# Storing raw z and its silu later, and passing q, k, v and 1/sum through DRAM in copies of 128 partitions

## The chip, the cores and the metric

The kernel runs on one core of a Trainium2 chip. The metric is the device time of one execution in microseconds (us). A core has a matrix engine (TensorE, PE in the profile, its weight loads PEld), a vector engine (VectorE, DVE), a scalar engine with lookup tables for functions such as exp and silu (ScalarE, ACT), a general engine (GpSimd, POOL) and SyncE (SP), which here only issues DMA copies. Sixteen DMA engines carry the copies between DRAM and the on-chip memory. Each engine follows its own list of instructions in order and waits for others by semaphores.

## The reference

One layer of a latent backbone, for 1,024 tokens (a grid of 16 rows by 64 columns), 256 context tokens, 1,024 features and 8 heads of 64, all in float32:

```python
h  = rmsnorm(x, norm_g) * (1 + scale) + shift          # scale, shift, gate from c and w_ada
hc = rmsnorm(ctx, norm_g) * (1 + scale_c) + shift_c
q, k, v, za, u, bg, cg, zc = jnp.split(h @ w_in, SPLIT_POINTS, axis=-1)     # 8 x 512 columns
kc, vc = jnp.split(hc @ w_in[:, D_ATTN:3 * D_ATTN], 2, axis=-1)
# q, k, kc: rmsnorm per head, q also rotated (axial rope) for the scores against k
# each query sees an 8 x 16 window of keys with a learned bias, and all 256 context keys
# without bias and with the unrotated q; one softmax over both
attn = neighbourhood_attention(q, k, v, kc, vc, rpb) * jax.nn.silu(za)
conv = bg * centred_short_conv(cg * u, conv_w, conv_b) * jax.nn.silu(zc)    # 3 taps
x_new = x + gate * (jnp.concatenate([attn, conv], axis=-1) @ w_out)
```

## The kernel before

Every product of matrices is done three times over (`mm3`): both operands are split into a high part and a rest, and high x high, high x rest and rest x high are added up. So q, k and v exist as two tensors each, index `l` (0 high, 1 rest). Work runs in four stages.

1. Modulation: `w_ada` is read, the gains and shifts are formed, x is normalised and turned so that features lie on partitions, and the products of the first group of the convolution are made.
2. Projection. The heads are handled in 4 pairs, 128 columns of q, k and v each. The loop `for n in range(NT + 3)` (L1170; NT = 32, a pair times a block of 128 tokens) issues one block's 24 matmuls into `pacc` and, behind it, the steps of the blocks before: normalisation, rotation, the transposes in `turn_qk` (L226) that put a pair's 2 x 64 head dimensions on the 128 partitions, and the stores. `turn_qk` stores q and k of two blocks at a time, `turn_kc` (L269) the context's keys and values. A store goes through `spill` into the list `stores`, which is emptied onto SP once a block. Each head has DRAM tensors of its own: `q_d[h]` holds q in both parts, rotated and plain, for 64 head dimensions, `k_d[h]` and `kc_d[h]` high part and rest of the keys, `v_d[h]` and `vc_d[h]` the values. So a pair's 128 partitions are stored by two copies of 64.
3. Attention. `quarter(n)` (L1066) runs for n = 0 to 35, four quarters a head and four more to finish. In one quarter, step by step, n's scores and context scores are made, n - 1's maxima are finished, n - 2's exponentials are taken, n - 3's products with v are summed. Scores have the keys on partitions; maxima over keys are found by transposes into `pmx`, `mx` before and `mg` after them. v has a column of ones behind its 64 (zeros in the rest), so that the same matmul gives the softmax's sums. `finish` (L1038) puts a half head's result into `o_d[p]` and its sums into `rs_d[p]`, by ScalarE's own queue.
   In between, TensorE does matmuls that attention doesn't need: the generator `fill` makes the z columns of the four head pairs (`attn_group`, L484), then three groups of the convolution (`conv_group`). `TICKS[n]` says how many portions go into quarter n; one portion is six matmuls of 512 columns into `pu`. Their weights come as `uraw` (two buffers, loaded a unit ahead by SP), are split on ScalarE (`uh`) and VectorE (`ul`). Work of theirs for ScalarE and VectorE is queued with `chore` and done at fixed places of a quarter by `do_acts` and `do_dves`.
   When a pair's last half is done, `gated(p)` (L1267) is made the current gating: a step in each quarter, run by `next(gating[0])`, inverts the sums by way of `ri_d[p]`, loads silu(z) (`zs`), the attention result (`tb`) and the inverse sums repeated over 64 partitions each (`rb`), multiplies, and stores `y_d[p]`. The last pair is gated in stage 4.
4. Output projection: `put_y` (L1334) loads the eight parts of y, `load_wo` the weights; 16 tiles of 24 matmuls into `pout`.

What a head loads for attention is asked for by `load_k`, `load_q` and `load_v` (from L944): the partitions 0 to 63 and 64 to 127 of `k_s` and of `kc_s` are both filled with the head's 64 rows, in which high part and rest of the keys lie side by side. `q_s` has the high part of q on partitions 0 to 63 and the rest on 64 to 127 (i below), and in its free dimension the rotated q ahead of the plain one (k below), so that one matmul multiplies a part of the keys with both parts of q:

```python
for i in range(2):
    rows = slice(64 * i, 64 * i + 64)
    for k in range(2):
        sp.dma_start(self.q[rows, k].bitcast(F32).rearrange("p (t c) -> p t c", c=256), q_d[h][i, :, :, k])
    sp.dma_start(self.kc[rows].bitcast(F32), kc_d[h])
```

So each tile of 128 partitions is filled by copies of 64. k and q have two sets of buffers, one for the even heads (`hcp`), one for the odd ones (`prp`). Head 0's k and q are loaded at the projection's blocks 26 and 27, each later head's during the head before: masks and q are asked for ahead of that head's quarter 1, k ahead of its quarter 2 (counted from 0), and v ahead of the own quarter 0.

In attention PE, ACT, DVE and POOL do their instructions in the order of the program (`strict`). The order on SP, and of all engines in the projection, is set by a scheduler that goes by a timing model of its own. All hardware copies of SP and ACT share eight semaphores.

Of the kernel before, what the change touches and what calls it, by code (L numbers as in the profile page):

```python
# [39 lines left out]
def body(tc, es, x, ctxt, w_ada, b_ada, w_in, q_g, k_g, rpbr, w_out, vecs, cst, out):  # L40
# [60 lines left out]
    zs_d = many("zs_d", NPAIR, [P, T])  # L101


    q_d = many("q_d", NH, [2, HD, 4, 2, 256])
    k_d = many("k_d", NH, [HD, 4, 2, 256])
    v_d = many("v_d", NH, [P, 4, 2, 2 * HD])
    kc_d = many("kc_d", NH, [HD, 2, L])
    vc_d = many("vc_d", NH, [P, 2, 2 * HD])
# [82 lines left out]

    def put_v(vs, i, ps):

        halves(vs[:, :, 0, i], vs[:, :, 1, i], ps.rearrange("p (s d) -> p s d", s=2))
# [31 lines left out]
    def turn_qk(pp, p, two, t0):  # L226
# [8 lines left out]
        def put():  # L235
# [4 lines left out]
            for s in range(2):  # L240
                h, rows = 2 * p + s, slice(64 * s, 64 * s + 64)
                for l in range(2):
                    spill(q_d[h][l, :, t0 // 2], qs[rows, l])
                spill(k_d[h][:, t0 // 2], ks[rows])
# [13 lines left out]
    def normed_ctx(pp, acc, scales):  # L258
        two = []
        vs = pp.tile([P, 2, 2, 2, HD], F32R, name="vs", tag="vs", bufs=4)  # L260
# [8 lines left out]
    def turn_kc(pp, p, two, vs):  # L269
# [4 lines left out]
        def put():  # L274
            ks = pp.tile([P, 2, 256], F32R, name="ks", tag="ks", bufs=2)
            halves(ks[:, 0], ks[:, 1], pB[:, :256])
            for s in range(2):
                h, rows = 2 * p + s, slice(64 * s, 64 * s + 64)
                spill(kc_d[h], ks[rows])
                spill(vc_d[h], vs[:, s].rearrange("p l i d -> p l (i d)"))  # L280
# [195 lines left out]

    def silus(z):
        out = []
        for half, ps in z:
            out.append(cvp.tile([P, 512], F32, name="zs", tag="ub", bufs=2))  # L480
            act.activation(out[half], ps, AF.Silu)
        return out

    def attn_group(f):  # L484

        z = []
        for got in unit(z_col(f)):
            if got:
                z.append(got)
            else:  # L490
                yield

        def on_act():
            for half, zs in enumerate(silus(z)):
                sp.dma_start(zs_d[f][:, half * 512:(half + 1) * 512], zs)
        chore(on_act)
# [8 lines left out]
    def load_sums(f, half, rb, queue):  # L505
        for i in range(2):
            queue.dma_start(rb[64 * i:64 * i + 64],
                            ri_d[f][i:i + 1, half * 512:(half + 1) * 512].broadcast_to([64, 512]))
# [426 lines left out]

    class head:
# [7 lines left out]
        def load_k(self):  # L944
            h = self.h
            self.k = self.place().tile([P, 4, 2, 256], F32R, name="k_s", tag="A")
            for i in range(2):
                sp.dma_start(self.k[64 * i:64 * i + 64].bitcast(F32), k_d[h])

        def load_q(self):  # L950
# [3 lines left out]
            for i in range(2):  # L954
                rows = slice(64 * i, 64 * i + 64)
                for k in range(2):
                    sp.dma_start(self.q[rows, k].bitcast(F32).rearrange("p (t c) -> p t c", c=256), q_d[h][i, :, :, k])
                sp.dma_start(self.kc[rows].bitcast(F32), kc_d[h])

        def load_v(self):  # L960
            h = self.h
            self.v = vts[h % 2]
            for l in range(2):
                for t in range(4):
                    sp.dma_start(self.v[:, l, 2 * t:2 * t + 2, 0:HD].bitcast(F32),
                                 v_d[h][:, t, l].rearrange("p (b d) -> p b d", d=HD))
                sp.dma_start(self.v[:, l, NB:, 0:HD].bitcast(F32), vc_d[h][:, l].rearrange("p (b d) -> p b d", d=HD))
# [98 lines left out]
    def quarter(n):  # L1066
# [17 lines left out]
        if gating and next(gating[0], "end"):  # L1084
            gating.clear()
# [5 lines left out]
        for i, hd_, j in now:  # L1091
            hd_.scores(j, sbank[:, i])
        if live(n):
# [11 lines left out]
        for _ in range(1):  # L1105
# [27 lines left out]
        for _ in range(ticks - 1):  # L1133
# [24 lines left out]
    sq = pp.tile([P, 4, HD + 1], F32, name="sq")  # L1158
    pool.memset(sq[:, :, HD:], EPS)
# [10 lines left out]
    for n in range(NT + 3):  # L1170
# [13 lines left out]
        if 9 <= n < 25 and n % 2:  # L1184
            next(tables)
        if n == NT - 6:
# [24 lines left out]
        if 0 < n <= NT:  # L1211
            scales[n - 1] = head_scale(pp, tiles[n - 1], 4)
            if n % 2:
                vs = pp.tile([P, 2, 2, 2, HD], F32R, name="vs", tag="vs", bufs=4)
# [228 lines left out]
```

## Time and profile before

| | before |
|---|---|
| median of 3 timed runs | 641.58 us (641.37 to 641.83) |
| profiled execution, whole | 643.59 us |
| its span, first to last instruction | 641.8 us |
| granted TensorE clock | 0.999 of full |
| TensorE busy | 629.1 us, 98% (weight loads 537.3 us, beside it) |
| VectorE busy | 432.3 us, 67% |
| ScalarE busy | 322.5 us, 50% |
| GpSimd busy | 131.5 us, 20% |
| SP's queue (q1) | 112,348 packets, 113.23 MB, 61.4% of 16 DMA engines |
| ScalarE's queue (q10) | 6,208 packets, 11.05 MB, 5.5% |
| DRAM read, written | 88.01 MB, 38.53 MB |

The profile is of one execution. Busy is time in which an engine carried out an instruction. An instruction made in a helper has the helper's line (L55), so that tiles' names tell the groups apart; `out<-in` names what is written and read. A wait is the idle time of an engine ahead of an instruction, put down to what ended it. A copy of so many rows is moved as that many packets or more, each by one of the sixteen DMA engines.

### The profile page before, as it was taken

Reading aid. Unit: us, or ns where it says so; the run is one execution under the profiler, and the core shown is the slowest. Engines: PE = TensorE matmul, PEld = TensorE weight load, DVE = VectorE, ACT = ScalarE, POOL = GpSimd, SP = SyncE. Lnnn points to the kernel's source line nnn. Section 1 sums busy time; section 2 is a strip of 40 time slices with the busy share of each in tenths; the row PEclk is TensorE's granted clock in tenths of the full one; section 3 lists DMA queues with packets and bytes.
Section 4 is the critical chain, followed back from the end, with each engine's and each line's share of the span. In section 5 each row is a group of like instructions: output and inputs, shape, how many; then the busy total and the mean of one; then the engine's idle time right before and its main releaser. Section 6 shows DMA issues by size and latency. Waiting matters only on the chain.

```text
span 641.8 us, 10295 instructions
## 1 busy us (share of the span) xinstructions
PE 629.1 (98%) x3480; PEld 537.3 (84%) x3480; DVE 432.3 (67%) x819; ACT 322.5 (50%) x692; POOL 131.5 (20%) x138
## 2 busy tenths in 40 slices
PE   8999999999999999999999999999999999999997
PEld 3477899999899999777688878888888888888885
DVE  1677859665756756458697889988998864565111
ACT  3676835424525444346676648565675644352000
POOL 1205024123123222001111211121111111004421
PEclk9999999999999999999999999999999999999999
DMA  8973647867785897899767758885862223965621
GB/s 319 379 257 97 180 121 259 256 188 206 241 260 165 271 269 218 216 221 223 184 160 195 186 140 212 202 214 149 225 150 88 71 81 128 293 235 198 215 100 49
DMA packets 118864, 125.46 MB, mean 195 GB/s; under 512 B 32817, under 2 KB 89353, under 8 KB 117532
## 3 DMA queue, kind: packets, MB, share of 16 engines
q1 hardware_dynamic: 112348, 113.23, 61.4%
q10 hardware_dynamic: 6208, 11.05, 5.5%
q0 software_dynamic: 256, 0.54, 0.3%
q8 instruction: 27, 0.44, 0.3%
q14 instruction: 25, 0.20, 0.1%
HBM read 88.01 MB, written 38.53 MB: 197 GB/s over the span
## 4 chain that ended last, share of the span: by engine, by line
PE 75%; DMA 10%; DVE 8%; SPq 3%; ACT 2%; issue 1%; ACTq 0%; DVEq 0%
PE pacc L55 21%; PE pu L55 18%; PE acc L55 5%; PE pout L76 5%; PE pout L74 5%; PE pout L75 5%; PE po L55 4%; PE tr L55 4%; PE cacc L55 4%; DMA v<-v_d 4%; DMA k_s<-k_d 3%; DVE mx L55 2%; DVE sb L55 2%; PE pss L55 2%; PE pmx L55 2%; DMA slab<-in_w_ada 2%
## 5 line engine op out<-in xcount | busy, mean ns | idle before, releaser
L55 PE MATMUL pu<-h,uh 128*128 128x512 f32 x544 | 169.0, 392 | 0.0
L55 PE MATMUL pacc<-wh,h 128*128 128x384 f32 x512 | 135.1, 338 | 0.0
L55 PEld LDWEIGHTS pu<-h,uh 128*128 128x128 f32 x544 | 98.2, 188 | 17.0
L55 PE MATMUL pu<-h,ul 128*128 128x512 f32 x272 | 106.3, 391 | 0.0
L55 PEld LDWEIGHTS pacc<-wh,h 128*128 128x128 f32 x512 | 92.8, 188 | 0.1
L55 POOL TENSOR_TENSOR plc<-sc,phc 128x512 fp32r<-128x512 f32 x32 | 42.5, 1327 | 222.8 <-ACT sc L55 111.4
L55 PE MATMUL pacc<-wl,h 128*128 128x384 f32 x256 | 85.6, 335 | 0.0
L55 POOL TENSOR_TENSOR ss<-ss,few 128x4 f32<-128x4 f32 (+1 forms) x40 | 42.0, 1051 | 125.8 <-DVE ss L55 125.4
L55 PEld LDWEIGHTS pu<-h,ul 128*128 128x128 f32 x272 | 51.1, 188 | 11.3
L55 DVE TENSOR_TENSOR mx<-mx,sb 128x384 f32<-128x384 f32 (+1 forms) x64 | 55.5, 876 | 1.9
L75 PE MATMUL pout<-wol,yh 128*128 128x512 f32 x128 | 49.8, 389 | 0.0
L76 PE MATMUL pout<-woh,yl 128*128 128x512 f32 x128 | 49.6, 389 | 0.0
L74 PE MATMUL pout<-woh,yh 128*128 128x512 f32 x128 | 48.3, 389 | 0.0
L55 PEld LDWEIGHTS pacc<-wl,h 128*128 128x128 f32 x256 | 48.1, 188 | 0.1
L55 DVE TENSOR_REDUCE ss<-sq 128x4 f32<-128x260 f32 (+1 forms) x40 | 15.7, 393 | 41.9 <-ACT sq L55 41.9
L55 ACT COPY mg<-pmx 128x256 f32<-128x256 f32 x32 | 12.0, 374 | 61.7 <-PE pmx L55 44.5
L55 ACT ACTIVATE sq<-pacc 128x256 f32<-128x256 f32 x32 | 12.3, 385 | 57.1 <-PE pacc L55 56.6
L1375 DVE TENSOR_TENSOR ot<-pout,gate 128x512 f32<-128x512 f32 x16 | 10.8, 688 | 37.6 <-PE pout L76 35.5
L55 DVE TENSOR_TENSOR pll<-sb,phl 128x768 fp32r<-128x768 f32 (+2 forms) x33 | 29.3, 889 | 7.9 <-ACT sb L55 7.9
L55 DVE TENSOR_TENSOR sc<-sc,mg 128x512 f32<-128x512 f32 x32 | 21.8, 683 | 19.0 <-ACT mg L55 19.0
L1376 POOL TENSOR_TENSOR ot<-ot,xr 128x512 f32<-128x512 f32 x15 | 20.0, 1347 | 67.6 <-DVE ot L1375 66.5
L55 ACT ACTIVATE qn<-pacc,ss 128x64 f32<-128x64 f32 x128 | 30.1, 329 | 4.7 <-issue 2.5
(151 smaller groups left out, 1277.0 us busy)
## 6 DMA issues: line engine op xcount, KB each, us to landing
uraw<-in_w_in SPq DMA_DIRECT2D x34, 256.0 KB
q_d<-qs SPq DMA_DIRECT2D x64, 128.0 KB
k_s<-k_d SPq DMA_DIRECT2D x16, 512.0 KB
q_s<-q_d SPq DMA_DIRECT2D x32, 256.0 KB
wr<-in_w_in SPq DMA_DIRECT2D x40, 192.0 KB
slab<-in_w_ada SPq DMA_DIRECT2D x6, 1024.0 KB
t_d<-btw SPq DMA_DIRECT2D x8, 576.0 KB
bt<-t_d SPq DMA_DIRECT2D x8, 576.0 KB
```

The costliest lines, as they stand in the source:

```text
L55: i = emit(*a, **kw)
L74: i = pe.matmul(ps, ah, bh, start=first, stop=False)
L75: pe.matmul(ps, ah, bl, start=False, stop=False)
L76: pe.matmul(ps, al, bh, start=False, stop=last)
L1375: dve.tensor_tensor(ot, ps, gate[:, cols], ALU.mult)
L1376: (dve if (nh, t) == (1, NB - 1) else pool).tensor_tensor(ot, ot, xr, ALU.add)
```

## The change

- z is stored as it comes from TensorE (`z_d`), by a copy on ScalarE for each half. Its silu is taken in the gating, on the loaded tile: the list `held` hands the tiles to the next `silus` call, that of a convolution group or, for pairs 1 and 2, one of its own (`chore(lambda: silus(()))`). The last pair's is taken in `put_y`.
- In the gating, z is loaded with the sums, two tiles at once, and the two products of a half are done in one step. A gating still running when the next pair is ready is no longer replaced but followed by it.
- `q_d`, `k_d`, `kc_d` and `v_d` belong to a pair and have 128 partitions, so that one copy stores a pair's q, or k, or context k. v is kept in the layout that attention reads, its columns of ones included; context v lies in the same tensor as the last two blocks. The ones and zeros are set once in three `vs` tiles of the projection rather than in the two `vts` tiles of attention.
- `load_k` and the `kc_s` load fill 128 partitions by one copy whose source runs over the head's 64 rows twice (`twice`). `load_q` makes two copies of 128 partitions instead of four of 64, `load_v` two instead of ten, and `load_sums` one instead of two.
- Quarter 0's first fill portion is put ahead of its context scores instead of behind them. An Exp on one column is put at the projection's block 29, ahead of attention.

The diff, without the hunk that takes `vs` from `next_vs` in `normed_ctx`:

```diff
@@ -98,14 +98,13 @@
     rs_d = many("rs_d", NPAIR, [2, 2, 512])
-    zs_d = many("zs_d", NPAIR, [P, T])
-    q_d = many("q_d", NH, [2, HD, 4, 2, 256])
-    k_d = many("k_d", NH, [HD, 4, 2, 256])
-    v_d = many("v_d", NH, [P, 4, 2, 2 * HD])
-    kc_d = many("kc_d", NH, [HD, 2, L])
-    vc_d = many("vc_d", NH, [P, 2, 2 * HD])
+    z_d = many("z_d", NPAIR, [P, T])
+    q_d = many("q_d", NPAIR, [2, P, 4, 2, 256])
+    k_d = many("k_d", NPAIR, [P, 4, 2, 256])
+    v_d = many("v_d", NPAIR, [P, 2, 2, NB + 2, HD + 1])
+    kc_d = many("kc_d", NPAIR, [P, 2, L])
     ri_d = many("ri_d", NPAIR, [2, T])
@@ -189,9 +188,18 @@
+    vss = []
+    def next_vs():
+        vss.append(vss.pop(0))
+        return vss[-1]
+    def spill_v(p, b, vs):
+        spill(v_d[p][:, :, :, b:b + 2].rearrange("p s l b d -> p (s l) (b d)"), vs.rearrange("p s l i d -> p (s l) (i d)"))
-        halves(vs[:, :, 0, i], vs[:, :, 1, i], ps.rearrange("p (s d) -> p s d", s=2))
+        halves(vs[:, :, 0, i, :HD], vs[:, :, 1, i, :HD], ps.rearrange("p (s d) -> p s d", s=2))
@@ -237,11 +245,9 @@
             halves(ks[:, 0], ks[:, 1], pB[:, :256])
-            for s in range(2):
-                h, rows = 2 * p + s, slice(64 * s, 64 * s + 64)
-                for l in range(2):
-                    spill(q_d[h][l, :, t0 // 2], qs[rows, l])
-                spill(k_d[h][:, t0 // 2], ks[rows])
+            for l in range(2):
+                spill(q_d[p][l, :, t0 // 2], qs[:, l])
+            spill(k_d[p][:, t0 // 2], ks)
         return put
@@ -274,10 +279,8 @@
             halves(ks[:, 0], ks[:, 1], pB[:, :256])
-            for s in range(2):
-                h, rows = 2 * p + s, slice(64 * s, 64 * s + 64)
-                spill(kc_d[h], ks[rows])
-                spill(vc_d[h], vs[:, s].rearrange("p l i d -> p l (i d)"))
+            spill(kc_d[p], ks)
+            spill_v(p, NB, vs)
         return put
@@ -474,26 +477,30 @@
+    held = []
             act.activation(out[half], ps, AF.Silu)
+        while held:
+            for v in held.pop():
+                act.activation(v, v, AF.Silu)
         return out
-        z = []
+        def keep(half, ps):
+            z = cvp.tile([P, 512], F32, name="z", tag="ub", bufs=2)
+            act.copy(z, ps)
+            sp.dma_start(z_d[f][:, half * 512:(half + 1) * 512], z)
             if got:
-                z.append(got)
+                chore(lambda got=got: keep(*got))
             else:
-        def on_act():
-            for half, zs in enumerate(silus(z)):
-                sp.dma_start(zs_d[f][:, half * 512:(half + 1) * 512], zs)
-        chore(on_act)
@@ -503,9 +510,8 @@
     def load_sums(f, half, rb, queue):
-        for i in range(2):
-            queue.dma_start(rb[64 * i:64 * i + 64],
-                            ri_d[f][i:i + 1, half * 512:(half + 1) * 512].broadcast_to([64, 512]))
+        r = ri_d[f]
+        queue.dma_start(rb, bass.AP(r.tensor, r.offset + half * 512, [[T, 2], [0, HD], [1, 512]]))
@@ -933,6 +939,12 @@
+    def twice(rows):
+        n = 1
+        for step, size in list(rows.ap)[1:]:
+            n *= size
+        return bass.AP(rows.tensor, rows.offset, [[0, 2], [n, HD], [1, n]])
@@ -944,27 +956,22 @@
             self.k = self.place().tile([P, 4, 2, 256], F32R, name="k_s", tag="A")
-            for i in range(2):
-                sp.dma_start(self.k[64 * i:64 * i + 64].bitcast(F32), k_d[h])
+            sp.dma_start(self.k[:].bitcast(F32).rearrange("p t l c -> p (t l c)"), twice(k_d[self.p][64 * self.s:64 * self.s + 64]))
             self.kc = bmp.tile([P, 2, L], F32R, name="kc_s", tag="kc_s", bufs=2)
-            for i in range(2):
-                rows = slice(64 * i, 64 * i + 64)
-                for k in range(2):
-                    sp.dma_start(self.q[rows, k].bitcast(F32).rearrange("p (t c) -> p t c", c=256), q_d[h][i, :, :, k])
-                sp.dma_start(self.kc[rows].bitcast(F32), kc_d[h])
+            for k in range(2):
+                sp.dma_start(self.q[:, k].bitcast(F32).rearrange("p (t c) -> p t c", c=256),
+                             q_d[self.p][:, 64 * self.s:64 * self.s + 64, :, k])
+            sp.dma_start(self.kc[:].bitcast(F32).rearrange("p l c -> p (l c)"), twice(kc_d[self.p][64 * self.s:64 * self.s + 64]))
             for l in range(2):
-                for t in range(4):
-                    sp.dma_start(self.v[:, l, 2 * t:2 * t + 2, 0:HD].bitcast(F32),
-                                 v_d[h][:, t, l].rearrange("p (b d) -> p b d", d=HD))
-                sp.dma_start(self.v[:, l, NB:, 0:HD].bitcast(F32), vc_d[h][:, l].rearrange("p (b d) -> p b d", d=HD))
+                sp.dma_start(self.v[:, l].bitcast(F32), v_d[self.p][:, self.s, l])
@@ -1082,7 +1089,7 @@
         if gating and next(gating[0], "end"):
-            gating.clear()
+            gating.pop(0)
         if live(e):
@@ -1090,6 +1097,9 @@
             hd_.scores(j, sbank[:, i])
+        if n == 0:
+            next(fill)
+            ticks -= 1
         if live(n):
@@ -1102,7 +1112,7 @@
             act.activation(w, w, AF.Exp)
-        for _ in range(1):
+        for _ in range(n > 0):
             next(fill, None)
@@ -1130,7 +1140,7 @@
             dve.tensor_tensor(pl, w, ph.bitcast(F32), ALU.subtract)
-        for _ in range(ticks - 1):
+        for _ in range(ticks - (n > 0)):
             next(fill, None)
@@ -1156,6 +1166,10 @@
     sq = pp.tile([P, 4, HD + 1], F32, name="sq")
+    vss += [pp.tile([P, 2, 2, 2, HD + 1], F32R, name=f"vs{i}")[:] for i in range(3)]
+    for v in vss:
+        for l in range(2):
+            pool.memset(v[:, :, l, :, HD:HD + 1].bitcast(F32), 1.0 - l)
     pool.memset(sq[:, :, HD:], EPS)
@@ -1183,6 +1197,8 @@
             next(tables)
+        if n == NT - 3:
+            act.activation(few[:, 5:6], ones, AF.Exp)
         if n == NT - 6:
@@ -1211,12 +1227,11 @@
             if n % 2:
-                vs = pp.tile([P, 2, 2, 2, HD], F32R, name="vs", tag="vs", bufs=4)
+                vs = next_vs()
             put_v(vs, (n - 1) % 2, tiles[n - 1][:, 256:384])
                 q, r = divmod(n - 1, NB)
-                for s in range(2):
-                    spill(v_d[2 * q + s][:, r // 2], vs[:, s].rearrange("p l i d -> p l (i d)"))
+                spill_v(q, r - 1, vs)
         if t == at + 1 and n < NT:
@@ -1258,9 +1273,6 @@
     fill_up(prp, 64)
-    for v in vts:
-        for l in range(2):
-            pool.memset(v[:, l, :, HD:HD + 1].bitcast(F32), 1.0 - l)
@@ -1268,21 +1280,29 @@
         sp.dma_start(ri, rs_d[f].rearrange("h b (x c) -> (h b x) c", c=16))
+        cols = [slice(half * 512, (half + 1) * 512) for half in range(2)]
+        zs = [ap.tile([P, 512], F32, name="zs", tag="zs", bufs=2) for _ in cols]
+        for v, c in zip(zs, cols):
+            sp.dma_start(v, z_d[f][:, c])
         yield
         sp.dma_start(ri_d[f].rearrange("h (x c) -> (h x) c", c=16), ri)
+        held.append(zs)
+        if f:
+            chore(lambda: silus(()))
         yield
-        for half in range(2):
-            cols = slice(half * 512, (half + 1) * 512)
-            zs, tb, rb = (ap.tile([P, 512], F32, name=n, tag=n, bufs=1) for n in ("zs", "tb", "rb"))
-            sp.dma_start(zs, zs_d[f][:, cols])
-            sp.dma_start(tb, o_d[f][:, cols])
+        while held:
+            yield
+        for v, c in zip(zs, cols):
+            tb, rb = (ap.tile([P, 512], F32, name=n, tag=n, bufs=1) for n in ("tb", "rb"))
+            half = cols.index(c)
+            sp.dma_start(tb, o_d[f][:, c])
             load_sums(f, half, rb, sp)
             yield
-            dve.tensor_tensor(zs, zs, rb, ALU.mult)
+            dve.tensor_tensor(v, v, rb, ALU.mult)
+            dve.tensor_tensor(tb, tb, v, ALU.mult)
+            sp.dma_start(y_d[f][:, c], tb)
             yield
-            dve.tensor_tensor(tb, tb, zs, ALU.mult)
-            sp.dma_start(y_d[f][:, cols], tb)
@@ -1303,9 +1323,13 @@
                 if p < NPAIR - 1:
-                    gating[:] = [gated(p)]
+                    gating.append(gated(p))
                 else:
                     recip(p, ap)
+        for step in gating:
+            for _ in step:
+                do_acts()
+                do_dves()
         for _ in fill:
@@ -1341,9 +1365,10 @@
                 rb = op.tile([P, 512], F32, name="rb", tag="rb", bufs=2)
-                act.dma_start(zs, zs_d[f][:, cols])
+                act.dma_start(zs, z_d[f][:, cols])
                 act.dma_start(tb, o_d[f][:, cols])
                 load_sums(f, half, rb, pool)
+                act.activation(zs, zs, AF.Silu)
                 dve.tensor_tensor(zs, zs, rb, ALU.mult)
```

More of the change, by code (lines that the diff above doesn't have):

```diff
@@ L258, in normed_ctx @@
     def normed_ctx(pp, acc, scales):
-        two = []
-        vs = pp.tile([P, 2, 2, 2, HD], F32R, name="vs", tag="vs", bufs=4)
+        two, vs = [], next_vs()
         for i in range(2):
@@ L1213, in body @@
             if n % 2:
-                vs = pp.tile([P, 2, 2, 2, HD], F32R, name="vs", tag="vs", bufs=4)
+                vs = next_vs()
             put_v(vs, (n - 1) % 2, tiles[n - 1][:, 256:384])
```

## The prediction

> **What bounds the kernel now.** I read the head of the page first, then TensorE's own waits, then the table of stretches.
>
> ```profile
> span 641.8 us, 10295 instructions
> PE 629.1 (98%) x3480; PEld 537.3 (84%) x3480; DVE 432.3 (67%) x819; ACT 322.5 (50%) x692; POOL 131.5 (20%) x138
> ```
> ```profile
> PE pmx L55 <- DVE mx L55: 1.9, 5, 0.7
> PE acc L55 <- POOL warm L55: 1.4, 1, 1.4
> PE pmx L55 <- DVE rm L55: 1.2, 5, 0.5
> PE pc L55 <- DVE qs L55: 1.1, 1, 1.1
> PE acc L55 <- ACT h L55: 0.8, 1, 0.8
> PE po L55 <- POOL plc L55: 0.6, 1, 0.6
> ...
> PE pmx L55 <- DMA uraw<-in_w_in: 0.2, 1, 0.2
> ```
> TensorE (PE) has work in 98% of the span. The columns of the second view are total wait, times, longest. The waits on pmx, pc and po belong to attention: 1.9 + 1.2 + 1.1 + 0.6 + 0.2 = 5.0 us. That is all that the change can win, for its matmuls are the same in number and, but for one tick of six, in order. What it can lose has no such limit, since it changes the copies that feed TensorE. So the copies are what I priced most closely.
>
> ```profile
> 10.00:15.00 5.00, 4.77 (x25) 1.82 (x23) 1.43 (x4) 3.19 (x5) 1.02 (x2) 1.00 1.04 410
> 224.00:271.00 47.00, 46.71 (x274) 44.30 (x272) 24.51 (x69) 21.00 (x77) 9.59 (x15) 1.00 0.88 235
> 271.00:485.00 214.00, 208.83 (x1190) 175.47 (x1191) 181.21 (x276) 137.70 (x225) 34.46 (x30) 1.00 0.76 189
> ```
> The last three columns are granted clock, DMA share and GB/s. The sixteen DMA engines are busy for 0.88 of the end of the projection and 0.76 of attention up to the last head. A DMA engine that does nothing but long reads moves 410 / 16 = 25.6 GB/s (first row); in attention a busy one moves 189 / (16 x 0.76) = 15.5 GB/s.
>
> **How a copy is spread over the engines.**
>
> ```profile
> q1 hardware_dynamic: 112348, 113.23, 61.4%
> q10 hardware_dynamic: 6208, 11.05, 5.5%
> woraw<-in_w_out ACTq DMA_DIRECT2D x16, 256.0 KB
> tb<-y_d ACTq DMA_DIRECT2D x14, 256.0 KB
> o_d<-ob ACTq DMA_DIRECT2D x16, 128.0 KB
> zs<-zs_d ACTq DMA_DIRECT2D x2, 256.0 KB
> tb<-o_d ACTq DMA_DIRECT2D x2, 256.0 KB
> rs_d<-ob ACTq DMA_DIRECT2D x16, 2.0 KB
> t_d<-t_d SPq DMA_DIRECT2D x16, 96.0 KB
> t_d<-in_rpb SPq DMA_DIRECT2D x8, 23.2 KB
> ```
> ScalarE's queue (q10) made 6,208 packets. Its copies have 128 rows (woraw, tb, zs: 34 copies), 64 rows (o_d: 16) or one row (rs_d: 16): 34 x 128 + 16 x 64 + 16 = 5,392 rows. The other 816 are 50 x 16 + 16 x 1: one closing packet for each engine used, sixteen for a tall copy, one for a single row. On q1 the rows of the 541 copies, counted from their shapes, are 103,931, which leaves 8,417 closing packets; 541 x 16 would be 8,656. The 239 missing ones come out exactly if a copy runs on the largest number up to 16 that divides its outermost count: the 24 t_d copies (outermost count 8 or 248) on 8 engines, which is 192; one of 56 rows on 14, 2; three of one row on one, 45. The sixteen t_d<-t_d copies are decisive: each has 64 rows, as 8 by 8, and ran on 8 engines. So the outermost count decides, not the number of rows.
>
> The Trainium skill, page "DMA: Bandwidth & Descriptors", section "Rules for kernel authors", states the same: an outermost dimension smaller than sixteen, such as a leading repeat of step zero, holds the whole copy to that many engines. By that rule the changed loads below run on two engines; the trace agrees for outermost counts of 8 and 1, and no row here has a 2 against a 128.
>
> **The loads: the term that decides.** After the change the source of q_s is `q_d[p][:, rows, :, k]`, outermost count 2 (high part and rest); k_s and kc_s read through `twice`, outermost `[0, 2]`; rb reads `[[T, 2], [0, HD], [1, 512]]`. All have 2 outermost against 128 in the tile. I take it that these run on two engines, one for each half of the partitions.
>
> ```profile
> k_s<-k_d SPq DMA_DIRECT2D x16, 512.0 KB
> q_s<-q_d SPq DMA_DIRECT2D x32, 256.0 KB
> kc_s<-kc_d SPq DMA_DIRECT2D x16, 128.0 KB
> rb<-ri_d SPq DMA_DIRECT2D x12, 128.0 KB
> ACT uh L55 <- DMA uraw<-in_w_in: 11.9, 3, 7.5
> ```
> ```profile
> 223.75 1.48 SPq L55 DMA_DIRECT2D k_s<-k_d  x2
> ...
> 457.19 1.24 SPq L948 DMA_DIRECT2D k_s<-k_d  x2
> ```
> ```profile
> 328.12 0.64 PE L55 MATMUL pc<-q_s,kc_s 128*128 128x256 f32 x4
> ...
> 482.43 0.64 PE L55 MATMUL pc<-q_s,kc_s 128*128 128x256 f32 x4
> ```
> A head brings 2 x 512 + 4 x 256 + 2 x 128 = 2,304 KB, 2.36 MB, before and after. On two engines that is 1.18 MB each, 46 us at 25.6 GB/s. A head now takes (482.4 - 328.1) / 5 = 30.9 us (the rows are the first quarters of heads 2 and 7). So loads that fit beside the matmuls no longer do: two engines become the bound of the stage.
>
> I add up what those two engines carry from the first K copy (224 us) until head 7's K has landed, which its first scores (482 us before) wait for.
> - Eight heads' loads: 8 x 46 = 368 us.
> - Their sixteenth of all else. Now an engine is busy for 47 x 0.88 + 214 x 0.76 = 204 us in this time. The loads are 8 x 2.36 / 16 = 1.18 MB of it, 76 us at 15.5 GB/s. The other 128 us shrink to 77 us if they ran at 25.6 GB/s. Four of the six rb copies come in this time, 256 KB each, 5 us on two engines: 20 us. So 97 to 148; I take 115, nearer the fast row, since the other engines are then mostly idle.
> - Idle time: a head's tiles are free when the head two before has ended its scores, in the first quarter of the head between. I allow 5 us for each of seven heads, 35 us; a quarter lasts 30.9 / 4 = 7.7 us, so the bounds are 0 and two quarters, 105 us.
>
> Sum: 224 + 368 + 115 + 35 = 742 us, where 482 us stood: 260 us later. What follows, head 7 and the output projection, keeps its length.
>
> Why nothing hides this: SP issues its copies in one order, and behind q_s and k_s stand the uraw weights of the fill matmuls, z_d, v and the stores of q and k. Each needs its part from the two engines, and these take their queue in order. The program also gives its hardware copies eight semaphores in turn and issues none before the one eight places ahead has landed, ScalarE's o_d and rs_d among them. ScalarE casts uraw in program order (row above: it waits for it already), and behind a late cast stand the next quarter's mg and sc, and then TensorE.
>
> **The other parts**, small beside that.
>
> ```profile
> 287.39 1.28 ACT L55 ACT_TABLE_LOAD   x1
> 288.69 1.08 ACT L55 ACTIVATE zs<-pu 128x512 f32<-128x512 f32 x2
> ...
> 290.55 1.28 ACT L55 ACT_TABLE_LOAD   x1
> ```
> ```profile
> 295.05 0.33 PE L55 MATMUL pmx<-ci,mx 128*128 128x128 f32 x1 [0.67 <-DVE mx L55]
> ```
> ```profile
> v<-v_d SPq DMA_DIRECT2D x64, 64.0 KB
> L55 DVE TENSOR_TENSOR tb<-tb,zs 128x512 f32<-128x512 f32 x6 | 4.1, 684 | 0.0
> ```
> - Raw z: Silus in the first ten quarters become copies, and the seven table loads of 1.28 us there become one, put ahead of attention; two pairs come back with the Silus of pairs 1 and 2 (quarters 21 and 29). One such group (1.28 + 1.08 + 1.28 = 3.6 us of ScalarE) ended in a wait of 0.67 us (row at 295.05). Three go, two come: nothing, or a gain of up to 2.1 us out of the pmx waits' 3.1.
> - Tick ahead of the first context scores: covers the pc wait, 1.1 us. Exp table loaded early: ends the po wait, 0.6 us.
> - Gating: both products in one step, 2 x 0.68 us of VectorE in one quarter instead of two. Nothing in sum; a quarter may be late by 0.7 us.
> - v with its ones: 80 copies in rows of 256 B become 16 in rows of 2,600 B; stores of q, k, kc, v halve in number. SP issues 367 copies instead of 541. These keep 128 or 512 outermost, so sixteen engines. They relieve SP, which is not where TensorE waits.
>
> Together -3.8 us if the loads stay spread, and covered entirely if they do not.
>
> **The sum.** The profiled execution took 643.6 us (span 641.8 and 1.8 around it); the three timed runs have a median of 641.6, 2.0 below. 643.6 + 260 - 2.0 = 901.6, say 902 us.
>
> **Rivals.**
> - *The loads stay on sixteen engines* (faster). Then only the small parts count: 641.6 - 3.8 = 638 us, at best 636.6 with all 5.0 us of waits gone. For it: no row has a copy with 2 on one side and 128 on the other, and an engine could be chosen by the tile's side. The Trainium skill's same table advises one transfer of 128 partitions in place of two halves; no run here shows that yet. Against it: t_d. It decides once a source's outermost 2 does not count. Chance 0.08.
> - *Only the step-zero repeats are held to two engines* (k_s, kc_s, rb), while q_s, whose 2 has a real step, is spread. K and kc are 1,280 KB, 26 us a head on two engines; q's 1.05 MB on sixteen adds 2.6 us. 8 x 28.2 = 226 instead of 368: 118 us late, 760 us. For it: a repeat is the odder pattern; against it: t_d's 8 had a real step. Chance 0.05.
> - *The change does not do what it says for time*: loads spread, and the doubled gating steps and returned Silus eat the 3.8 us: 642 us. Chance 0.01.
>
> **How the numbers follow.** Forecast 0.86, rivals 0.08, 0.05, 0.01. A measurement here can tell about 0.2%, 1.3 us. Slower 0.86 + 0.05 = 0.91, same 0.01, faster 0.08. Within the forecast the floor is 224 + 368 + 97 - 482 = 207 us, 849; a rate a little above that five-microsecond mean would take some more off. The far end, 15.5 GB/s on the two engines with all other bounds, is 8 x 76 + 148 + 105 + 224 - 482 = 603 us, 1245; but that rate was seen with all engines at work, so I stop where 20 GB/s (59 us a head), 130 and 60 us lead: 404 us, 1046. The range 810 to 1050 leaves out the three rivals and some of the far end, about 2 in 10.
>
> **What would show it.** In the profile of the changed kernel: DMA share in attention falls to two or three tenths and GB/s to under 90, while TensorE, ScalarE and SP wait for q_s, k_s or uraw; the chain of waits is mostly DMA; K copies of neighbouring heads are issued some 60 us apart. The count is the sharpest test: 90,619 rows, and closing packets 367 x 16 - 239 - 38 x 14 = 5,101, so q1 has 95,720 packets; with sixteen engines throughout it has 96,252. If the count says two and the time is below 800, the idle and queueing terms are wrong; if it says sixteen, the forecast falls.

## The result and the profile after

The changed kernel takes 897.94 us (median of 4 runs, 897.23 to 899.8); the kernel before, on the same chip, 641.71 us (641.37 to 642.55). The ratio is 1.3995, 95% interval 1.3969 to 1.402: 256 us slower. The forecast was 902 us. In the experiments below, the times of b_k2, a_k2 and b_k2_pool leave out the executions more than 1.5% above that kernel's fastest; the texts on record ahead of the runs go by the median of all four of b_k2, 783 us.

The head of the page, of the changed kernel, with its queues (packets, MB, share of sixteen engines):

```profile
span 896.0 us, 10021 instructions
PE 662.6 (74%) x3479; PEld 564.3 (63%) x3480; DVE 430.0 (48%) x819; ACT 324.5 (36%) x699; POOL 130.8 (15%) x138
...
q1 hardware_dynamic: 95720, 113.38, 38.0%
q10 hardware_dynamic: 6208, 11.05, 3.9%
```

TensorE worked in 98% of the span and now does in 74%. q1 has 95,720 packets, to the packet what the prediction gave for loads on two engines (sixteen would have made 96,252). The trace's semaphore events show the engines directly as well, one arrival for each engine that carried a part, and one more count right behind the issue where these are fewer than sixteen. Each `uraw` copy has sixteen arrivals, each `t_d` copy that the prediction put on eight engines has eight, and each of the 38 loads has two (K's of 372.58 us at 409.87 and 410.50 us). The bytes of q1 are the same within 0.2%, yet the queue's share fell from 61.4% to 38.0%. The longer span alone would make it 61.4 x 641.8 / 896.0 = 44.0%; the rest is that its packets are fewer and take less time, those of 8 KB 322 ns in the mean instead of 582 (from the first K copy to head 7).

The same stretches as in the prediction (last columns: granted clock, DMA share, GB/s); the second is attention up to the last head:

```profile
224.00:271.00 47.00, 30.94 (x179) 30.27 (x177) 10.88 (x32) 11.31 (x40) 6.39 (x8) 0.86 0.22 80
307.00:710.00 403.00, 227.50 (x1157) 190.71 (x1155) 167.53 (x259) 127.56 (x213) 33.70 (x29) 0.78 0.28 94
```

A share of 0.28 is 4.5 of sixteen engines busy, where it was 0.76. Two of them carry the loads, the others stand idle for most of the time. The waits of TensorE, of ScalarE, and the issues of K by SP:

```profile
PE pmx L55 <- DVE mx L55: 117.8, 12, 32.4
PE pss L55 <- DMA k_s<-k_d: 35.9, 3, 16.0
PE pu L55 <- DVE cv L55: 29.7, 1, 29.7
PE trA L55 <- DVE qs L55: 23.6, 1, 23.6
```
```profile
ACT uh L55 <- DMA uraw<-in_w_in: 140.1, 8, 36.2
ACT mg L55 <- DMA q_s<-q_d: 54.1, 4, 19.4
```
```profile
305.40 10.70 SPq L959 DMA_DIRECT2D k_s<-k_d  x1
372.58 10.76 SPq L959 DMA_DIRECT2D k_s<-k_d  x1
439.97 1.25 SPq L959 DMA_DIRECT2D k_s<-k_d  x1
485.09 11.08 SPq L959 DMA_DIRECT2D k_s<-k_d  x1
...
676.85 10.27 SPq L959 DMA_DIRECT2D k_s<-k_d  x1
```

The largest wait of TensorE is put down to VectorE (`mx`), but VectorE itself waits ahead of it for ScalarE (89.5 us for `uh`, 81.6 us for `mg`, rows below), and ScalarE waits for the weights `uraw` (140.1 us) and, ahead of `mg`, for its own issues of `rs_d` and `o_d` to come behind q_s (54.1 us). So what is late at TensorE is seldom the slow load itself: it is what queues behind it. SP mostly spends over 10 us on the one K issue of a head, where both halves together took it 1.1 to 1.5 us before. All its issues together took it 509 us instead of 287, though they are 367 instead of 541. The two rows of VectorE:

```profile
L55 DVE TENSOR_TENSOR ul<-uraw,uh 128x512 fp32r<-128x512 f32 x34 | 22.9, 684 | 89.6 <-ACT uh L55 89.5
...
L55 DVE TENSOR_TENSOR sc<-sc,mg 128x512 f32<-128x512 f32 x32 | 21.9, 684 | 81.6 <-ACT mg L55 81.6
```

One piece of the chain of waits, from K's issue at 372.58 to its landing, and the scores that follow:

```profile
372.58 37.92 DMA k_s<-k_d
410.50 0.04 issue
410.54 1.22 PE pss L55 x4
```

### The profile page after: what moved, and what is told of

Read it like the earlier page. It is cut to its first block, busy times and chain, and to the rows that moved or that the text cites. A ratio compares the mean times of both kernels' runs of the same rounds, so it can differ in the third digit from the quotient of the medians.

```text
span 896.0 us, 10021 instructions
## 1 busy us (share of the span) xinstructions
PE 662.6 (74%) x3479; PEld 564.3 (63%) x3480; DVE 430.0 (48%) x819; ACT 324.5 (36%) x699; POOL 130.8 (15%) x138
## 3 DMA queue, kind: packets, MB, share of 16 engines
q1 hardware_dynamic: 95720, 113.38, 38.0%
## 4 chain that ended last, share of the span: by engine, by line
PE 48%; DMA 31%; SPq 12%; DVE 4%; ACT 2%; issue 1%; ACTq 0%; DVEq 0%
PE pacc L55 13%; PE pu L55 10%; DMA k_s<-k_d 8%; DMA uraw<-in_w_in 5%; SPq L55 5%; PE acc L55 4%; DMA q_s<-q_d 4%; SPq L966 4%; DMA y_d<-tb 3%; PE pout L75 3%; PE pout L76 3%; PE pout L74 3%; DMA z_d<-z 3%; PE tr L55 3%; PE cacc L55 3%; DMA v_d<-vs 2%
## 5 line engine op out<-in xcount | busy, mean ns | idle before, releaser
L55 PE MATMUL pu<-h,uh 128*128 128x512 f32 x544 | 174.8, 403 | 29.7 <-DVE cv L55 29.7
L55 PE MATMUL pacc<-wh,h 128*128 128x384 f32 x512 | 137.9, 344 | 0.0
L55 PEld LDWEIGHTS pu<-h,uh 128*128 128x128 f32 x544 | 102.2, 196 | 47.6 <-DVE cv L55 29.9
L55 PE MATMUL pmx<-ci,mx 128*128 128x128 f32 x64 | 17.2, 323 | 126.3 <-DVE mx L55 117.8
L55 PEld LDWEIGHTS pmx<-ci,mx 128*128 128x128 f32 x64 | 9.5, 151 | 136.5 <-ACT sb L55 73.9
L55 ACT CAST uh<-uraw 128x512 fp32r<-128x512 f32 x34 | 20.8, 615 | 140.1 <-DMA uraw<-in_w_in 140.1
L55 DVE TENSOR_TENSOR ul<-uraw,uh 128x512 fp32r<-128x512 f32 x34 | 22.9, 684 | 89.6 <-ACT uh L55 89.5
L55 PE MATMUL pss<-q_s,k_s 128*128 128x384 f32 (+1 forms) x128 | 34.7, 401 | 35.9 <-DMA k_s<-k_d 35.9
L55 DVE TENSOR_TENSOR sc<-sc,mg 128x512 f32<-128x512 f32 x32 | 21.9, 684 | 81.6 <-ACT mg L55 81.6
L55 DVE TENSOR_TENSOR mx<-mx,sb 128x384 f32<-128x384 f32 (+1 forms) x64 | 51.0, 806 | 2.0
L55 PEld LDWEIGHTS pss<-q_s,k_s 128*128 128x128 f32 x128 | 25.3, 237 | 36.8 <-issue 30.4
L55 ACT COPY mg<-pmx 128x256 f32<-128x256 f32 x32 | 11.9, 372 | 100.7 <-DMA q_s<-q_d 54.1
```

Source lines behind the costliest of these rows:

```text
L55: i = emit(*a, **kw)
```

## The experiments

All times are medians; ratios are to executions of the kernel before, taken side by side (median 642 to 643 us), so that they differ by up to 1% from the quotients of the medians. The kernels' names in the table below are used from here on.

| run | what has 2 outermost | us | ratio (95%) | q1 packets |
|---|---|---|---|---|
| changed kernel | k_s, kc_s, q_s, rb | 897.9 | 1.3995 (1.3969 to 1.402) | 95,720 |
| a_halves | nothing | 642.4 | 0.9988 (0.9968 to 1.0009) | 96,860 |
| a_interleaved | nothing, copies of 128 | 637.7 | 0.9919 (0.9898 to 0.994) | 96,348 |
| b_interleaved | nothing, loads alone | 642.0 | 1.0002 (0.9991 to 1.0014) | 111,836 |
| a_only_rb | rb | 650.3 | 1.0127 (1.0099 to 1.0155) | 96,680 |
| a_only_k | k_s | 719.9 | 1.1199 (1.1175 to 1.1223) | 96,620 |
| a_only_q | q_s | 763.9 | 1.1893 (1.1856 to 1.1929) | 96,380 |
| b_k2 | K, two copies of 64 | 775.5 | 1.2065 (1.1995 to 1.2135) | 112,124 |
| b_k8 | K, with 8 | 669.9 | 1.043 (1.0397 to 1.0463) | 112,220 |
| a_k2 | K, two copies of 64 | 743.3 | 1.1661 (1.1608 to 1.1713) | 96,636 |
| b_k2_pool | K, two copies of 64 | 757.9 | 1.1743 (1.1654 to 1.1832) | 112,124 |
| a_pool | all four | 899.0 | 1.3983 (1.3952 to 1.4014) | 95,720 |
| a_interleaved_pool | nothing | 638.1 | 0.994 (0.9924 to 0.9956) | 96,348 |

b_k2, b_k8, a_k2 and b_k2_pool read K's features in an order other than q's, so that their scores are of mismatched features; instructions and bytes stay the same.

**The loads undone (a_halves).**

```diff
-            sp.dma_start(self.k[:].bitcast(F32).rearrange("p t l c -> p (t l c)"), twice(k_d[self.p][64 * self.s:64 * self.s + 64]))
+            for i in range(2):
+                sp.dma_start(self.k[64 * i:64 * i + 64].bitcast(F32), k_d[self.p][64 * self.s:64 * self.s + 64])
...  (q_s, kc_s and rb likewise)
```

> The changed kernel with only the four loads written as before: k_s, q_s, kc_s and rb each filled by copies of 64 partitions out of the new pair tensors, outermost count 64 or 256 instead of 2. Theory A (an outermost count of 2 holds a copy to two DMA engines): 638 us, between 636.6 and 641.6; the q1 queue then has 90,619 rows and 405 x 16 - 239 = 6,241 closing packets, 96,860. Rival B (the pair tensors, raw z or the wide v copies slow the kernel): still near 898 us, or at least over 660. Rival D (the small parts cost as much as they save): 641 to 645 us.

642.4 us, and 96,860 packets. The whole loss is in the four loads. The small parts together bring nothing that can be told from zero in this form, where 3.8 us were forecast: for them rival D was right and theory A's 638 us was not reached.

**Still 128 partitions, but another count outermost (a_interleaved).**

```diff
-    q_d = many("q_d", NPAIR, [2, P, 4, 2, 256])
+    q_d = many("q_d", NPAIR, [P, 2, 4, 2, 256])
...
-                             q_d[self.p][:, 64 * self.s:64 * self.s + 64, :, k])
+                             q_d[self.p][64 * self.s:64 * self.s + 64].rearrange("d l t k c -> (d l) t k c")[:, :, k])
...
-        return bass.AP(rows.tensor, rows.offset, [[0, 2], [n, HD], [1, n]])
+        return bass.AP(rows.tensor, rows.offset, [[n, HD], [0, 2], [1, n]])
```

> The changed kernel, its loads still one copy of 128 partitions, but with high part and rest of a feature on neighbouring partitions (2d and 2d + 1): K's source is [64 rows][twice][row] and q's is 128 rows in a line, so that the outermost counts are 64 and 512. rb by two copies of 64. Theory A: 638 us (636.6 to 641.6), and 90,619 rows + 373 x 16 - 239 = 96,348 packets on q1. Rival E (a copy that reads each row twice is slow in any order, at two engines): K and kc at 25 us a head on two engines, about 700 us (660 to 760), and 224 packets fewer.

637.7 us. Each row of K is still read twice by one copy, with a step of zero; only the repeat has moved from the outermost place to the second, and each of its K and q copies now has sixteen arrivals. That is 260 us apart from the changed kernel. A repeat costs nothing where 64 stands ahead of it, so rival E falls. This is also the version that beats both kernels. Its queue, and that of a_halves, with the same bytes:

```profile
q1 hardware_dynamic: 96348, 113.38, 54.2%
```
```profile
q1 hardware_dynamic: 96860, 113.38, 59.5%
```

One copy of 128 partitions takes less of the engines than two of 64 (54.2% against 59.5%). What TensorE waits for in attention fell from the 5.0 us of the prediction to 1.8 + 0.9 = 2.7 us in a_halves and 0.9 + 0.5 = 1.4 us here (271 to 485 us of a_halves, then of a_interleaved). The profiled execution of a_halves is the shortest of its twelve, 639.5 us, so what the median one lost is not in this trace:

```profile
PE pmx L55 <- DVE mx L55: 1.8, 4, 1.1
PE pmx L55 <- DVE rm L55: 0.9, 3, 0.5
```
```profile
PE pmx L55 <- DVE rm L55: 0.9, 3, 0.5
PE pmx L55 <- DVE mx L55: 0.5, 2, 0.3
```

**The wide loads alone (b_interleaved).** The loads of a_interleaved, on the kernel before, whose `q_d` then has the rows of a head in the order [HD, 2, 4, 2, 256].

> The kernel before (silu ahead of storing, heads' own tensors, narrow v copies) with only the loads of a_interleaved: q_d rows in the order feature, then part; k_s, kc_s and q_s each by copies of 128 partitions with outermost counts 64 and 512. 509 copies on q1: 103,931 rows + 509 x 16 - 239 = 111,836 packets. If the wide loads make the gain of a_interleaved: 638 to 639 us. If raw z, wide v and pair stores make it: 642 to 643 us, as a_halves has them and stood at 0.9988 of before.

642.0 us, no gain, although its q1 share is 56.3% against 61.4%. a_halves has the rest without the wide loads: no gain either. Only both together gain: 5 us, with runs that stay within 636.9 and 638.2, where a_halves spread from 639.5 to 646.1. The Trainium skill, page "DMA: Bandwidth & Descriptors", section "Rules for kernel authors", advises one transfer of 128 partitions in place of two halves; the queue's shares agree with it twice (59.5% to 54.2%, 61.4% to 56.3%), the time only together with the rest of the change. In the trace of b_interleaved the waits on `pmx` and `pc` are still those of before (2.1 + 1.2 + 1.1 us). Why the two parts gain only together is not shown further.

**Outermost 2 and 8 without a repeat, in the kernel before (b_k2, b_k8).** Only K's load is changed, for b_k2 so (8 and 8 for b_k8):

```diff
+                kd = k_d[h]
-                sp.dma_start(self.k[64 * i:64 * i + 64].bitcast(F32), k_d[h])
+                sp.dma_start(self.k[64 * i:64 * i + 64].bitcast(F32).rearrange("p t l c -> p (t l c)"),
+                             bass.AP(kd.tensor, kd.offset, [[2048, 2], [2 * 2048, 32], [1, 2048]]))
```

> The kernel before, with one thing changed: the 64 rows of K are read as 2 groups of 32 (even rows, then odd ones), a real step, no repeat, still two copies of 64 partitions with rows of 8 KB. The features of K so come in another order, and the scores are of mismatched features; the work is the same. Theory A: two engines carry K, 128 rows x 309 ns / 2 = 19.8 us a head, with 3.6 us for their part of q and kc and 11.8 us for all else as in the changed kernel: 35.2 us against 30.8 us a head, 4.4 x 7.5 = 33 us, so 675 us (642 to 700), and 112,348 - 16 x 14 = 112,124 packets on q1. Rival C (only step-zero repeats are held to two engines): 642 us and 112,348 packets.

> As b_k2 with 8 groups of 8 rows (mismatched features again). Theory A: eight engines, 5 us a head each: 642 us (641 to 644), and 112,348 - 16 x 8 = 112,220 packets on q1. Rival F (any source whose rows are not in one line is held back, whatever the count): as b_k2, and by its packets.

Both packet counts are met to the packet (112,124 and 112,220), and each K copy has two arrivals in b_k2 and eight in b_k8, so the outermost count sets the number of engines with a real step as with a repeat; rivals C and F fall. The rule of the same section of the Trainium skill, that a small outermost dimension confines a copy, agrees for 2 and for 8. Both times were missed: 776 us instead of 675, 670 instead of 642. The sum of what the two engines carry explains 33 us of b_k2's 775.5 - 643.0 = 132; what makes b_k8's 27 us was not tried apart. In the trace of b_k2, the second of one head's K copies (issued by SP at 379.10) and what ScalarE does meanwhile:

```profile
379.10 30.57 DMA k_s<-k_d
```
```profile
386.80 0.56 ACT L55 COPY ob<-po 65x512 f32<-65x512 f32 x1
399.67 0.21 ACTq L1044 DMA_DIRECT2D rs_d<-ob  x1
409.69 0.45 ACTq L1045 DMA_DIRECT2D o_d<-ob  x1
410.24 0.37 ACT L55 COPY mg<-pmx 128x256 f32<-128x256 f32 x1 [22.88 <-DMA k_s<-k_d]
```

K lands 30.6 us after its issue. ScalarE's store of `o_d` leaves at 409.69, as K lands, and `mg`, which TensorE's next steps need, comes 22.88 us late. This is the turn of eight semaphores: the trace gives each copy's semaphore, the copies of SP and ScalarE have eight between them (100, 101, 103 to 108), and this store has 103, as the K copy of 379.10 had. SP too stands still: behind the K copies of another head it spends 18.47 us on two `uraw` issues:

```profile
328.78 1.13 SPq L949 DMA_DIRECT2D k_s<-k_d  x2
330.34 5.26 SPq L967 DMA_DIRECT2D v<-v_d  x2
335.69 18.47 SPq L295 DMA_DIRECT2D uraw<-in_w_in  x2
```

That is not the turn. The first of these two has semaphore 100, and the copy that had it before, a part of q_s issued at 326.00, had landed by 332.2; still the issue, begun at 335.69, lasts 8.39 us, where an `uraw` issue took 0.38 us (median) in the kernel before. What holds such an issue is not shown. It comes with confined copies: SP has 29 issues of over 2 us in b_k2 and 49 in the changed kernel, and 2 each in the kernel before and in a_interleaved. That these engines take their queue in order shows in the `v` copy issued at 330.34: fourteen of its arrivals were there by 337.85, the last two came at 356.61 and 358.48, just behind the second K copy's two at 356.42 and 358.27.

**Which of the queued copies costs (b_k2_pool, a_pool).** `rs_d` and `o_d` are issued by GpSimd's queue.

```diff
-            act.dma_start(rs_d[self.p][self.s, bank:bank + 1], ob[64:65])
-            act.dma_start(o_d[self.p][64 * self.s:64 * self.s + 64, bank * 512:(bank + 1) * 512], ob[0:64])
+            pool.dma_start(...)  (both)
```

> b_k2 (K's rows as 2 groups of 32 on the kernel before, mismatched features) with rs_d and o_d issued by GpSimd's queue instead of ScalarE's, so that they no longer take one of the eight semaphores that the hardware copies use in turn. In b_k2 ScalarE stood still ahead of mg for 46.7 + 22.9 + 22.2 = 92 us with such an issue. A2 (those issues wait for the K copy eight places earlier, and what ScalarE does next comes late): 783 falls by most of 92, to 700 us (670 to 725). Rival G (K itself lands too late: 30 us from issue, against 25 us of lead in the kernel before): stays over 750. Load alone (A1) would have given 675 for both.

> The changed kernel, all four loads with outermost 2, with rs_d and o_d issued by GpSimd's queue. The two engines carry 425 us of loads and rb and about 100 us of the rest between 222 and 730 us, all of that time: by load (A1) there is nothing to win, 895 us (875 to 915). A2 (the wait of ScalarE's issues is what costs): falls by its 54 us ahead of mg or more, 840 us or less.

b_k2_pool: 758 us. ScalarE's waits ahead of `mg` for a DMA are gone from the trace, 92 us of them, but only 775.5 - 757.9 = 18 us came back: it now waits for `uraw` instead, 67.8 us after 34.1 us, and TensorE waits for K itself 25.0 us, after 11.9 us:

```profile
ACT uh L55 <- DMA uraw<-in_w_in: 67.8, 8, 19.5
```
```profile
PE pss L55 <- DMA k_s<-k_d: 25.0, 3, 11.6
```

So A2 is a part and not the price. G's figure ("over 750") came, but its cause, K's late landing, is 25.0 us at TensorE; the larger wait in this trace is ScalarE's for `uraw`, whose issues on SP last up to 11 us here, as in b_k2. a_pool: 899 us, no gain, as A1 said: with all four loads on them the two engines are the bound, and the waits taken from ScalarE's issues come back as waits for `uraw` (184.2 us instead of 140.1).

**One load at a time, in the changed kernel (a_only_q, a_only_k, a_only_rb).** As a_halves, with one of the loads left as the change has it.

> The changed kernel with k_s, kc_s and rb by copies of 64 partitions again; only q_s keeps its outermost count of 2 (a real step, no repeat). Rival C (only step-zero repeats are confined): 640 us and 389 x 16 - 239 = 5,985 closing packets, 96,604 on q1. Theory A, 5,761 closing packets, 96,380. Price by load alone (A1): q 8,192 packets x 46 ns / 2 engines / 8 heads = 23.6 us a head, 3.2 for k and kc, 12.5 for the rest: 39.3 against 30.8 us, 8.5 x 7.5 = 64, so 704 us (680 to 720). Price by what waits behind a slow copy (A2): the K-only kernel paid 140 us for 19.8 us a head, so q costs 140 x 23.6 / 19.8 = 167, 807 us (760 to 830).

> The changed kernel with q_s and rb by copies of 64 partitions; k_s and kc_s keep the leading step-zero 2. Theory A: 96,380 packets on q1. Price by load alone (A1): k and kc (329 + 90) us / 2 engines / 8 = 26.2 us a head, 3 for q, 12.5 for the rest: 41.7 against 30.8 us, 10.9 x 7.5 = 82, so 720 us (700 to 740). Price by what waits behind a slow copy (A2): 140 x 26.2 / 19.8 = 185, 825 us (780 to 840).

> The changed kernel with k_s, q_s and kc_s by copies of 64 partitions; only rb keeps the outermost 2, six copies on SP and two on GpSimd's queue. 96,860 - 6 copies fewer x 16 - 6 x 14 = 96,680 packets on q1. By load: 128 packets x 84 ns / 2 = 5.4 us for each copy, 11 us in one head of two: hidden within the 30.8 us, so 642 us (639 to 648). If each of the six stands in the way in full: 642 + 32 = 674 us.

The second text is mistaken in its first sentence: the kernel that ran keeps the leading 2 in k_s alone, kc_s comes by halves, so that the 720 us which it gives for A1 are of another kernel. The count is then 90,619 + 397 x 16 - 239 - 8 x 14 = 96,620, which was measured, and by the same steps A1 gives 20.6 + 3.6 + 12.5 = 36.7 us a head, 686 us, and A2 642 + 140 x 20.6 / 19.8 = 788 us. The 720 us lie between, as the 764 us of q_s do between 704 and 807. q_s has a real step and no repeat, and it costs more than K: rival C falls again. rb costs 650.3 - 642.4 = 8 us, a quarter of the 32 us that six copies fully in the way would. Against a_halves, K costs 77 us, q 121 and rb 8, 207 together; the four at once cost 255.5. kc_s was not tried alone, and whether it makes the other 50 us or the parts add up to more than their sum stays open.

**Two copies of 64 or many copies of v (a_k2).** a_halves with K's load of b_k2.

> a_halves (every load by copies of 64 partitions) with K's rows as 2 groups of 32, as b_k2 has them (mismatched features): two copies of K a head on two engines, but v in two wide copies a head instead of ten narrow ones. With K alone on two engines the changed kernel with one copy of 128 took 720 us and b_k2, the same bytes in two copies of 64, 783. V (the many narrow v copies that stand behind K in the turn of eight semaphores make the 63 us): 720 us (705 to 740). H (two copies of 64 instead of one of 128 make it): 783 us (760 to 800). Packets on q1 either way 96,860 - 16 x 14 = 96,636.

743 us, between the two. The same bytes of K on two engines cost 77 us as one copy of 128 (a_only_k), 101 as two of 64 (a_k2), and, with the narrow v copies and the rest of the kernel before, 132 against that kernel (b_k2). Neither V nor H alone is right; each seems to hold for about a half, and that split is not shown by more than these three runs.

**ScalarE's issues, where the loads are spread (a_interleaved_pool).** The edit of a_pool on a_interleaved.

> a_interleaved with rs_d and o_d issued by GpSimd's queue, which takes them out of the turn of eight semaphores. If ScalarE's issues still hold TensorE up where the loads are spread: 637 us or a little less (its waits in attention are 1.4 us in all). If not, GpSimd's share costs: 637.7 to 640 us.

638.1 us (637.6 to 639.3) against 637.7 (636.9 to 638.2): nothing to gain there.

## Why the prediction was right

The step that decided was that a source with 2 outermost runs on two DMA engines. It was read from the packet counts of the trace before, where outermost counts of 8 and 1 appeared, and it holds for 2: 95,720 packets, and the counts of eight more kernels were foretold to the packet (that of a_only_k was not, for the reason given). a_halves and a_interleaved show that nothing else in the change costs the time.

The terms of the sum, against the trace of the changed kernel, from the first K copy (222.9 us) to head 7's first context scores:

```profile
730.41 1.05 PE L55 MATMUL pc<-q_s,kc_s 128*128 128x256 f32 x4
```

- The loads: 46 us a head were forecast from 25.6 GB/s. K's 1,024 packets took 322 ns in the mean, q's 8,192 took 46.2, kc's 1,024, of 2 KB, are put at the median of that size, 84: 330 + 378 + 86 = 794 us, on two engines 397 us, 49.6 a head instead of 46.
- All else: 115 us were taken, rb's 20 in it. The packets of this time sum up to 2,429 us; less the loads and the four rb copies of this time (4 x 128 x 84 ns = 43 us) that is 1,592 us, a sixteenth of it 100 us, and 22 for rb on two engines: 122 us.
- Idle time: 35 us were allowed, of bounds 0 to 105. The two terms above make 519 us, and the time was 507 us. So by this sum there was none; packets overlap on an engine a little, up to 23 were under way at once.
- Together 518 us were forecast for what took 507.
- What follows head 7 was to keep its length. It grew by 6 us (896.0 - 730.4 = 165.6, against 641.8 - 482.4 = 159.4). TensorE is busy for 158.1 us of it instead of 154.9, at a granted clock of 0.92 in the first 10 us, and waits 2.5 us where it waited for nothing before, 1.9 of them for the weights `woh` of the output projection. rb on GpSimd's queue takes 13.9 us from issue to landing, where its halves took 3.7. That wait for `woh` stands in the other two kernels with 2 outermost in rb as well (a_only_rb 2.6 us, a_pool 2.1 us) and not in a_halves, a_only_q, a_only_k or a_k2; the steps between rb and `woh` were not followed:

```profile
rb<-ri_d POOLq DMA_DIRECT2D x2, 256.0 KB, 13.9
```

So 12 us too many up to head 7, 6 too few behind it, and 2 taken off for the distance between profiled and timed executions, which here is nearly nothing (897.75 and 897.94), make the 4 us between forecast and result. The mechanism and its price are right; that they agree to half a per cent is luck, since errors of up to 35 us in the terms cancel. Two signs came out otherwise: GB/s, forecast under 90, is 94 in the trace, and the chain of waits, forecast to be mostly DMA, is DMA for 251 of the 507 us and SP's issuing for another 107 (17 us in the same stage before). The prediction names SP's order, but not that an issue itself would last; its sum comes out without a term for it. K's issues were to stand some 60 us apart, and stood 45 to 82 apart.

The small parts were forecast at -3.8 us with spread loads (638 us). a_interleaved took 637.7, but not for the reasons given: a_halves has the same small parts without that gain. The term that was left at nothing, the shape of the copies, decides there whether the other parts show. That 638 was met is luck.

What the method would have got wrong is the price of one load alone. There the sum of an engine's work says 675, 686 and 704 us, and the chip 776, 720 and 764. In these runs the sum holds only where the two engines have no idle time left. Short of that the kernel waits for latencies: K may be asked for only when the head two before it is done, and must land before the next head's scores. The prediction's paragraph on what queues behind the loads names most of these waits, but gave them no price of their own.

## What to carry to other kernels

Before a copy is made wider, look at the outermost count of its source, the side that was tried here, and put the 64 or 128 rows there; a repeat belongs second. Test it by the packets: a copy leaves one closing packet for each engine that it uses, so that the count of a queue tells the spread without any timing, as the arrivals at a copy's semaphore do. Price a slow copy by its load only if the engines are full; else look at the chain from its earliest possible issue to its last user, at the other copies that may not start until it has landed, and at how long their issues last; no run here tests a price made that way.

## What was not expected

The granted clock of TensorE followed its idleness. It was 0.999 of full before, and 0.868 in the changed kernel: 0.78 between 307 and 710 us, where TensorE worked in 56% of the time, 0.87 up to 790 us (78%) and 0.98 from there on (93%). With the same matmuls but for one lost record TensorE is busy for 662.6 us instead of 629.1, 33 us more. In a_interleaved, with TensorE at work in 99% of the span, it is 0.999 again. A kernel that waits is slowed in its matmuls as well; how much of the 33 us lay beside copies that were later still is not shown.
